# Transposes moved from TensorE to VectorE and block transfers in a two-layer hybrid trunk

## The chip, the cores and the metric

The kernel runs on one core of one Trainium2 chip. The metric is the device time of one execution in microseconds (us). Engines are called TensorE (PE in the profile; PEld is its weight load), VectorE (DVE), ScalarE (ACT), GpSimd (POOL) and SyncE (SP).

## The reference

The reference runs two layers over x, 256 tokens by 2048 channels, all in float32. Each layer computes, from one normalised input h:

```
h    = rms_norm(x) * norm_g
proj = h @ w_in                    # c_q, c_kv, k_rope, z_a, u, v, z_b, q_c, k_c, v_c, a_r, z_c, gates
y_a  = attention(c_q, c_kv, k_rope) * silu(z_a)   # 8 heads, 128 + 64 rotary, RMSNorm of q and k, causal softmax
y_b  = gelu(u) * (tril(w_s) @ rms_norm(gelu(v)) + b_s) * silu(z_b)   # inside chunks of 128 tokens
y_c  = rms_norm(gla(q_c, k_c, v_c, a_r)) * silu(z_c)   # gated linear attention, 4 heads, chunks of 128
merged = sum over the three branches of sigmoid(gate_b) * (y_b @ w_branch[b])
x    = x + merged @ w_out
```

## The kernel before

**Weights and blocks.** A projection block is 256 tokens by 512 output columns. Its contraction is cut into pieces of 128, and a weight chunk is two of these: 128 partitions by 1024 float32, 512 KB. `Weights.chunk` loads a chunk on SP's queue into `wraw` (four buffers), ScalarE rounds it into `whi` (L65), VectorE puts the rest into `wlo` (L66), three buffers each. `block` then makes three matmuls of 128x512 for each piece and each half of the tokens: high input by high weight (L207), high by low (L208), low by high (L209), so twelve to a chunk. The inputs need the same split: xT (the layer's input), cT (the normalised latents), yTa, yTb, yTc (the branch outputs) and mT (merged) all hold a transposed input in a high and a low half.

**A layer** runs through 320 chunks in this order: c_q and c_kv (32), z_a (32, behind a narrow block), q from cT0 (6), k and v of attention from cT1 (4 + 4), then q_c, k_c, v_c, z_c, v, u, z_b, the gates, the branch projections, and w_out. In the text these are counted as chunk positions from the layer's start: q begins at 34, the value block of attention ends at 48, q_c runs from 48 to 56, v begins at 96, u at 112. A layer has 320, so the second begins at 320.

**Transposes.** There are two ways to turn a block. `transpose_split` uses TensorE: `transpose2` (L242) makes four transposes of 128x128 into PSUM, ScalarE and VectorE split the result. Each block of 512 columns takes eight of them. `move_split`, used for the branch outputs, turns 32x32 squares on VectorE (L277, two instructions a block) and then moves the squares to their places with 16 transfers on SP's queue (L281, 32 KB each, 32 partitions by 8 runs of 128 bytes). Attention turns its queries and keys with `transpose2` as well, into qTn and kTn (heads' 128 columns), qTr (rotary queries) and kTz (rotary keys, zero in the other half of the partitions); so does the gated linear attention for qkT.

**Work between the matmuls.** Short pieces of work (transposes, attention, the gated linear attention) are written as generators in a list; `block` calls `step()` after every three matmuls, which carries the first piece on to its next `yield`. `pause(n)` lets n steps go by. A scheduler then settles each engine's order from the program order and from priorities; weight loads and splits have a raised priority. Every engine, and every queue of transfers, takes its instructions in that order, and one that waits holds up those behind it.

**Names that the text uses.** `attention` makes `scores` (psc, from kTz with qTr and kTn with qTn), `turn` and `values`. `rsqrt` (L124 on VectorE makes m, L126 on GpSimd makes r by a power) makes the norms r_q and r_k. krs is the rotary key scaled by r_k. `gla` has eight levels: VectorE's `factors` makes X, TensorE's `plv` multiplies its halves, VectorE writes the result into AT; `po` is its output.

Of the kernel before, what the change touches and what calls it, by code (L numbers as in the profile page):

```python
# [71 lines left out]
def trunk(ctx: ExitStack, tc: tile.TileContext, a, out):  # L72
# [252 lines left out]
    for l in range(DEPTH):  # L325
# [101 lines left out]
        qn = t8("qn").rearrange("p (t c) -> p t c", t=NT)  # L427
        qr = t4("qr").rearrange("p (t c) -> p t c", t=NT)
        for j in range(3):
            acc = block(lq, 4)  # L430
            for t in range(NT):
                dst = qn[:, t, j * 512:(j + 1) * 512] if j < 2 else qr[:, t, :]
                act(dst, acc[t], AF.Copy, scale=rc[:, t:t + 1])
        kn = t8("kn").rearrange("p (t c) -> p t c", t=NT)
        vv = t8("vv").rearrange("p (t c) -> p t c", t=NT)
        for j in range(4):
            acc = block(lk, 4)
            for t in range(NT):
                dst = (kn if j < 2 else vv)[:, t, (j % 2) * 512:(j % 2 + 1) * 512]
                act(dst, acc[t], AF.Copy, scale=rc[:, 2 + t:3 + t])  # L440
        ssq, ssk = ts("ssq", 32), ts("ssk")
        for t in range(NT):
            for src, dst in ((qn, ssq[:, t * 8:(t + 1) * 8]), (kn, ssk[:, t * 8:(t + 1) * 8])):
                sq = t4("sq")
                act(sq, src[:, t, :], AF.Square)
                V.tensor_reduce(dst, sq.rearrange("p (h d) -> p h d", h=NH), AX.X, ALU.add)
            sq = t2("sqr")
            act(sq, qr[:, t, :], AF.Square)
            V.tensor_reduce(ssq[:, 16 + t * 8:16 + (t + 1) * 8], sq.rearrange("p (h d) -> p h d", h=NH),
                            AX.X, ALU.add)  # L450
            V.tensor_scalar(ssk[:, t * 8:(t + 1) * 8], ssk[:, t * 8:(t + 1) * 8], sskr[:, t:t + 1], None, ALU.add)
        V.tensor_tensor(ssq[:, 0:16], ssq[:, 0:16], ssq[:, 16:32], ALU.add)
        rq = rsqrt(ssq[:, 0:16], 16, 1.0 / 192, "q")
        rk = rsqrt(ssk[:, 0:16], 16, 1.0 / 192, "k")
        rqs = ts("rqs")
        V.tensor_scalar(rqs, rq, SCALE, None, ALU.mult)

# [467 lines left out]
```

## Time and profile before

| | |
|---|---|
| time, median of 3 runs | 1863.21 us (1862.96 to 1863.21) |
| the profiled execution | 1863.55 us, of which the span of the core's instructions 1861.8 us |
| mean granted TensorE clock | 1.0 |
| TensorE matmul / weight load busy | 99% / 83% |
| VectorE / ScalarE / GpSimd busy | 60% / 50% / 2% |
| mean traffic of the transfers | 194 GB/s |

Busy shares are means over the span. TensorE takes its matmuls one after the other, and a record's duration overlaps the next one's start; so what a group of matmuls costs is read from the distance between starts. Instructions that issue a transfer are not counted as busy, on GpSimd and SyncE neither.

### The profile page before, as it was taken

The page shows a single profiled execution, that of the slowest core. Times are in us where ns is not written, and L with a number is a line of the kernel's source. Part 1 is how long each engine was busy: PE and PEld are TensorE (multiplying, and loading weights), DVE is VectorE, ACT ScalarE, POOL GpSimd, SP SyncE. Part 2 cuts the span into 40 slices and gives each one's busy share as a digit, 9 for nine tenths or more (in the row PEclk, how much of TensorE's full clock was granted, in tenths as well). Part 3 has the DMA queues.
Part 4 walks back from the last instruction along what each step waited for, and adds up shares of the span by engine and source line. Part 5 has one row for each costly group of instructions (what it writes and reads, how often), then busy time and mean ns, then how long its engine had stood idle before and what let it go on. Part 6 is the DMA issues. An engine that isn't in the chain of part 4 may idle for free.

```text
span 1861.8 us, 22708 instructions
## 1 busy us (share of the span) xinstructions
PE 1850.6 (99%) x8504; PEld 1537.8 (83%) x8504; DVE 1107.8 (60%) x1436; ACT 932.2 (50%) x1174; POOL 43.6 (2%) x49
## 2 busy tenths in 40 slices
PE   8999999999999999999999999999999999999999
PEld 7888888888888888888888888888888888888887
DVE  5656558866455545465556665688664555554654
ACT  6765446554444444444547644455544444444443
POOL 0002000000000000000000010000000000000000
PEclk9999999999999999999999999999999999999999
DMA  8554564475576555575655545645755765556654
GB/s 319 188 189 156 175 209 170 147 214 183 192 209 199 192 192 192 192 235 195 212 197 185 192 146 183 205 167 158 214 176 196 211 199 190 194 187 207 220 201 158
DMA packets 150607, 360.51 MB, mean 194 GB/s; under 512 B 63456, under 2 KB 64128, under 8 KB 149984
## 3 DMA queue, kind: packets, MB, share of 16 engines
q1 hardware_dynamic: 146400, 346.30, 56.0%
q0 software_dynamic: 2656, 10.37, 1.7%
q10 hardware_dynamic: 1440, 2.39, 0.4%
q8 instruction: 66, 1.08, 0.2%
q14 instruction: 45, 0.37, 0.1%
HBM read 348.52 MB, written 4.19 MB: 189 GB/s over the span
## 4 chain that ended last, share of the span: by engine, by line
PE 96%; DVE 1%; issue 1%; ACT 1%; POOL 1%; DMA 0%; ACTq 0%; DVEq 0%
PE acc L208 30%; PE acc L207 30%; PE acc L209 30%; PE ptr L242 2%; PE plv L670 1%; DVE wlo L66 1%; PE ppv L555 1%; PE psc L524 1%; PE psc L520 1%; POOL r_q L126 1%; PE pmx L767 0%; PE po L693 0%; PE ppt L545 0%; DMA first_in<-in_gx 0%; PE accT L221 0%
## 5 line engine op out<-in xcount | busy, mean ns | idle before, releaser
L66 DVE TENSOR_TENSOR wlo<-wraw,whi 128x1024 fp32r<-128x1024 f32 (+1 forms) x642 | 782.3, 1219 | 682.2 <-ACT whi L65 681.6
L65 ACT ACTIVATE whi<-wraw 128x1024 fp32r<-128x1024 f32 (+1 forms) x642 | 677.8, 1056 | 787.0 <-PE acc L209 762.6
L207 PE MATMUL acc<-whi,xT 128*128 128x512 f32 x1792 | 704.0, 393 | 5.8 <-ACT whi L65 5.8
L208 PE MATMUL acc<-wlo,xT 128*128 128x512 f32 x1792 | 699.6, 390 | 1.5 <-DVE wlo L66 1.4
L209 PE MATMUL acc<-whi,xT 128*128 128x512 f32 x1792 | 698.6, 390 | 0.0
L207 PEld LDWEIGHTS acc<-whi,xT 128*128 128x128 f32 x1792 | 337.1, 188 | 73.7 <-ACT whi L65 5.8
L208 PEld LDWEIGHTS acc<-wlo,xT 128*128 128x128 f32 x1792 | 337.2, 188 | 71.5 <-DVE wlo L66 3.8
L209 PEld LDWEIGHTS acc<-whi,xT 128*128 128x128 f32 x1792 | 337.0, 188 | 70.0
L207 PE MATMUL acc<-whi,mT 128*128 128x512 f32 x256 | 100.0, 391 | 0.0
L209 PE MATMUL acc<-whi,mT 128*128 128x512 f32 x256 | 99.7, 389 | 0.0
L208 PE MATMUL acc<-wlo,mT 128*128 128x512 f32 x256 | 99.6, 389 | 0.0
L209 PEld LDWEIGHTS acc<-whi,mT 128*128 128x128 f32 x256 | 48.1, 188 | 10.1
L207 PEld LDWEIGHTS acc<-whi,mT 128*128 128x128 f32 x256 | 48.1, 188 | 9.8
L208 PEld LDWEIGHTS acc<-wlo,mT 128*128 128x128 f32 x256 | 48.1, 188 | 9.8
L207 PE MATMUL acc<-whi,yTa 128*128 128x512 f32 x128 | 50.0, 390 | 0.0
L209 PE MATMUL acc<-whi,yTa 128*128 128x512 f32 x128 | 49.8, 389 | 0.0
L208 PE MATMUL acc<-wlo,yTa 128*128 128x512 f32 x128 | 49.8, 389 | 0.0
L207 PE MATMUL acc<-whi,yTb 128*128 128x512 f32 x128 | 49.8, 389 | 0.0
L208 PE MATMUL acc<-wlo,yTb 128*128 128x512 f32 x128 | 49.8, 389 | 0.0
L209 PE MATMUL acc<-whi,yTb 128*128 128x512 f32 x128 | 49.8, 389 | 0.0
L207 PE MATMUL acc<-whi,yTc 128*128 128x512 f32 x128 | 49.8, 389 | 0.0
L208 PE MATMUL acc<-wlo,yTc 128*128 128x512 f32 x128 | 49.8, 389 | 0.0
(236 smaller groups left out, 1439.9 us busy)
## 6 DMA issues: line engine op xcount, KB each, us to landing
wraw<-in_w_big SPq DMA_DIRECT2D x634, 512.0 KB, 3.3
whole<-part SPq DMA_DIRECT2D x192, 32.0 KB, 3.3
x<-x POOLq DMA_DIRECT2D x8, 512.0 KB, 4.4
x<-in_x SPq DMA_DIRECT2D x2, 1024.0 KB, 8.9
wsT<-in_w_sT POOLq DMA_DIRECT2D x2, 1024.0 KB, 5.7
x<-in_x POOLq DMA_DIRECT2D x4, 512.0 KB, 5.3
out<-x ACTq DMA_DIRECT2D x8, 256.0 KB, 4.7
xTraw<-in_gx SPq DMA_DIRECT2D x3, 512.0 KB, 7.6
```

The costliest lines, as they stand in the source:

```text
L65: nc.scalar.activation(hi[:, c], raw[:, c], AF.Copy)
L66: nc.vector.tensor_tensor(lo[:, c], raw[:, c], hi[:, c].bitcast(F32), ALU.subtract)
L126: nc.gpsimd.tensor_tensor(r[:, :n], m[:, :n], neghalf[:, :n], ALU.pow)
L207: nc.tensor.matmul(o, xh[:, c], wh, start=kt + k == 0, stop=False)
L208: nc.tensor.matmul(o, xh[:, c], wl, start=False, stop=False)
L209: nc.tensor.matmul(o, xl[:, c], wh, start=False, stop=kt + k == kts - 1)
L242: nc.tensor.transpose(p[:, k * S + t * P:k * S + (t + 1) * P], src[:, t, (b + k) * P:(b + k + 1) * P], ident)
L520: nc.tensor.matmul(p3[:, :, 0:nk], qTr[:, c:c + P], z[:, h0 % 4:h0 % 4 + 2, 0:nk], start=True, stop=False)
L524: nc.tensor.matmul(p3[:, k, 0:nk], qTn[:, h * S + i * P:h * S + (i + 1) * P], kTn[:, h * S:h * S + nk], start=False, stop=k == 1)
L555: nc.tensor.matmul(po[:, (h - hh) * P:(h - hh + 1) * P], pT[:, k:k + P], vv[:, j, h * P:(h + 1) * P], start=j == 0, stop=j == i)
L670: nc.tensor.matmul(p[:, h * P:(h + 1) * P], X[:, 0, h, :], X[:, 1, h, :], start=True, stop=True)
```

## The change

All `transpose_split` blocks but two kinds are replaced by moves: VectorE's two transposes and 16 transfers. A new helper `move` does this with the queue as a parameter. cT0, cT1, mT0 to mT2 of each layer, xT0 to xT2 of the second layer, and qkT go by SP's queue; qTn, qTr, kTz and kTn of attention by GpSimd's. The last merged block (mT3) and the last input block (xT3) stay on TensorE. q, k and v of attention are evicted in another order of code, the rotary keys lie in kTz0 (even heads) and kTz1 (odd heads), the rotary part of a score pair is two matmuls of half the width, and qTn is scaled in place by ScalarE before the first score. Attention's generator begins with `pause(48)` instead of the transposes, the pairs run through the first four heads first, and the branch and gate weights are laid out in the order gate0, gate1, branch0, branch1, gate2, branch2, gate3, branch3. The `squares` helper holds the sums of squares that stood in line before.

```diff
@@ -266,22 +266,32 @@
         work.append(steps())
         return dst
-    def move_split(src, scale, name):
-        dst, part, whole = t8(name, F32R), t4("part"), t4("whole")
-        dv = dst.rearrange("p (h n) -> p h n", h=2)
-        blocks = part.rearrange("p (n i b) -> p n i b", n=8, i=4)
-        w4 = whole.rearrange("p (n j b) -> p n j b", n=8, j=4)
+    def move(dst, src, queue=nc.sync):
+        part = t4("part")
         for t in range(NT):
             V.transpose(part.rearrange("p (k t c) -> p k t c", k=4, t=NT)[:, :, t, :],
                         src[:, t, :].rearrange("p (k c) -> p k c", k=4))
+        pv = part.rearrange("p (n i b) -> p n i b", n=8, i=4)
+        dst = dst if isinstance(dst, list) else [dst, dst]
+        dv = [d.rearrange("p (n j b) -> p n j b", n=8, j=4) for d in dst]
         for j in range(4):
             for i in range(4):
-                nc.sync.dma_start(w4[32 * i:32 * i + 32, :, j, :], blocks[32 * j:32 * j + 32, :, i, :])
-        for k in range(4):
-            c = slice(k * S, (k + 1) * S)
-            split(dv[:, 0, c], dv[:, 1, c], whole[:, c], scale(k) if callable(scale) else scale)
+                queue.dma_start(dv[i // 2][32 * i:32 * i + 32, :, j, :], pv[32 * j:32 * j + 32, :, i, :])
+    def move_split(src, scale, name):
+        dst, whole = t8(name, F32R), t4("whole")
+        dv = dst.rearrange("p (h n) -> p h n", h=2)
+        move(whole, src)
+        if callable(scale):
+            for k in range(4):
+                c = slice(k * S, (k + 1) * S)
+                split(dv[:, 0, c], dv[:, 1, c], whole[:, c], scale(k))
+        else:
+            split(dv[:, 0], dv[:, 1], whole, scale)
         return dst
@@ -362,7 +372,7 @@
-        cT = [transpose_split(cl[j], lambda k, j=j: gain(l, 16 + 4 * j + k), f"cT{j}") for j in range(2)]
+        cT = [move_split(cl[j], lambda k, j=j: gain(l, 16 + 4 * j + k), f"cT{j}") for j in range(2)]
@@ -465,49 +446,81 @@
...
+        qkg = ts("qkg", 1)
+        V.tensor_tensor(qkg, gain(l, 24), gain(l, 25), ALU.mult)
+        qn = t8("qn").rearrange("p (t c) -> p t c", t=NT)
+        qr = t4("qr").rearrange("p (t c) -> p t c", t=NT)
+        qTn = t8("qTn")
+        for j in range(3):
+            acc = block(lq, 4)
+            for t in range(NT):
+                dst = qn[:, t, j * 512:(j + 1) * 512] if j < 2 else qr[:, t, :]
+                act(dst, acc[t], AF.Copy, scale=rc[:, t:t + 1])
+            if j < 2:
+                move(qTn[:, j * 1024:(j + 1) * 1024], qn[:, :, j * 512:(j + 1) * 512], nc.gpsimd)
...
+        qrr, qrt = t4("qrr"), t4("qrt")
         rotate(v4(qrr), v4(qrt), qr.rearrange("p t (h d) -> p t h d", h=NH), 0, NH)
+        qTr = t4("qTr")
+        move(qTr, qrr.rearrange("p (t c) -> p t c", t=NT), nc.gpsimd)
...
+        kn = t8("kn").rearrange("p (t c) -> p t c", t=NT)
+        for j in range(2):
+            acc = block(lk, 4)
+            for t in range(NT):
+                act(kn[:, t, j * 512:(j + 1) * 512], acc[t], AF.Copy, scale=rc[:, 2 + t:3 + t])
+        ssk = ts("ssk")
+        squares(ssk[:, 0:16], kn)
+        for t in range(NT):
+            V.tensor_scalar(ssk[:, t * 8:(t + 1) * 8], ssk[:, t * 8:(t + 1) * 8], sskr[:, t:t + 1], None, ALU.add)
+        rk = rsqrt(ssk[:, 0:16], 16, 1.0 / 192, "k")
+        rk4 = rk.rearrange("p (t h) -> p t h", t=NT)
         krs = t4("krs")
...
         V.tensor_tensor(v4(krs), v1(krr).broadcast_to([P, NT, NH, 64]),
                         rk4.unsqueeze(3).broadcast_to([P, NT, NH, 64]), ALU.mult)
...
+        kTz = [t4("kTz0"), t4("kTz1")]
+        nc.gpsimd.memset(kTz[0][64:128, :], 0.0)
+        nc.gpsimd.memset(kTz[1][0:64, :], 0.0)
+        move(kTz, krs.rearrange("p (t c) -> p t c", t=NT), nc.gpsimd)
+        kTn = t8("kTn")
+        for j in range(2):
+            half = kn[:, :, j * 512:(j + 1) * 512]
+            for t in range(NT):
+                kf = half[:, t, :].rearrange("p (h d) -> p h d", h=4)
+                V.tensor_tensor(kf, kf, rk4[:, t, 4 * j:4 * j + 4].unsqueeze(2).broadcast_to([P, 4, P]), ALU.mult)
+            move(kTn[:, j * 1024:(j + 1) * 1024], half, nc.gpsimd)
+        vv = t8("vv").rearrange("p (t c) -> p t c", t=NT)
+        for j in range(2):
+            acc = block(lk, 4)
+            for t in range(NT):
+                act(vv[:, t, j * 512:(j + 1) * 512], acc[t], AF.Copy, scale=rc[:, 2 + t:3 + t])
+        for j in range(2):
+            act(qTn[:, j * 1024:(j + 1) * 1024], qTn[:, j * 1024:(j + 1) * 1024], AF.Copy, scale=qkg)
         lsum = ts("lsum")
         ya = t8("ya").rearrange("p (t c) -> p t c", t=NT)
         def attention():
-            yield from pause(16)
-            for g in range(2):
-                b = 4 * g
-                z = kTz[g].rearrange("p (h s) -> p h s", h=4)
-                nc.gpsimd.memset(z[64:128, 0::2, :], 0.0)
-                nc.gpsimd.memset(z[0:64, 1::2, :], 0.0)
-                pq, pk = transpose2(qrr3, b // 2), transpose2(krs3, b // 2)
-                act(qTr[:, b // 2 * S:(b // 2 + 2) * S], pq, AF.Copy)
-                pk = pk.rearrange("p (h s) -> p h s", h=2)
-                V.tensor_copy(z[0:64, 0::2, :], pk[0:64])
-                act(z[64:128, 1::2, :], pk[64:128], AF.Copy)
-                yield
-                for b in (4 * g, 4 * g + 2):
-                    pq, pk = transpose2(qn, b), transpose2(kn, b)
-                    act(qTn[:, b * S:(b + 2) * S], pq, AF.Copy, scale=qkg)
-                    V.tensor_copy(kTn[:, b * S:(b + 2) * S], pk)
-                    yield
+            yield from pause(48)
             def scores(i, h0):
@@ -515,14 +528,13 @@
...
-                z = kTz[h0 // 4].rearrange("p (h s) -> p h s", h=4)
-                c = h0 // 2 * S + i * P
-                nc.tensor.matmul(p3[:, :, 0:nk], qTr[:, c:c + P], z[:, h0 % 4:h0 % 4 + 2, 0:nk],
-                                 start=True, stop=False)
+                c = h0 // 2 * S
                 for k in range(2):
                     h = h0 + k
+                    nc.tensor.matmul(p3[:, k, 0:nk], qTr[:, c + i * P:c + (i + 1) * P], kTz[k][:, c:c + nk],
+                                     start=True, stop=False)
                     nc.tensor.matmul(p3[:, k, 0:nk], qTn[:, h * S + i * P:h * S + (i + 1) * P],
-                                     kTn[:, h * S:h * S + nk], start=False, stop=k == 1)
+                                     kTn[:, h * S:h * S + nk], start=False, stop=True)
...
-            pairs = [(i, h) for i in range(NT) for h in (0, 2, 4, 6)]
+            pairs = [(i, h) for g in (0, 4) for i in range(NT) for h in (g, g + 2)]
@@ -607,6 +619,8 @@
+        for j in range(2):
+            move(qkT[:, j], qk[:, j])
@@ -622,11 +636,6 @@
-            for j in range(2):
-                ps = [transpose2(qk[:, j], hp * 2) for hp in range(2)]
-                for hp in range(2):
-                    act(qkT[:, j, hp * 512:(hp + 1) * 512], ps[hp], AF.Copy)
-                yield from pause(2)
@@ -801,18 +810,19 @@
                     else:
                         V.scalar_tensor_tensor(g[:, t, :], g[:, t, :], 1.0, acc[t], ALU.add, ALU.mult)
                         V.tensor_tensor(m[:, t, :], m[:, t, :], g[:, t, :], ALU.add)
-            mT.append(transpose_split(m, 0.5, f"mT{nb}"))
+            return m
         gate_block(0)
         finish()
         yT[1] = [move_split(uz[:, :, j * 512:(j + 1) * 512], 1.0, f"yTb{j}") for j in range(2)]
         gate_block(1)
-        merge_block(0)
+        for nb in range(2):
+            mT.append(move_split(merge_block(nb), 0.5, f"mT{nb}"))
         gate_block(2)
-        merge_block(1)
+        m = merge_block(2)
         gate_block(3)
-        merge_block(2)
-        merge_block(3)
+        mT.append(move_split(m, 0.5, "mT2"))
+        mT.append(transpose_split(merge_block(3), 0.5, "mT3"))
         lm = hl(mT)
@@ -833,7 +843,8 @@
-                xT.append(transpose_split(x, lambda k, l=l, nb=nb: gain(l + 1, 4 * nb + k), f"xT{nb}"))
+                turn = move_split if nb < 3 else transpose_split
+                xT.append(turn(x, lambda k, l=l, nb=nb: gain(l + 1, 4 * nb + k), f"xT{nb}"))
@@ -866,7 +877,7 @@
-        for f, nb in ((gate, 0), (gate, 1), (branch, 0), (gate, 2), (branch, 1), (gate, 3), (branch, 2), (branch, 3)):
+        for f, nb in ((gate, 0), (gate, 1), (branch, 0), (branch, 1), (gate, 2), (branch, 2), (gate, 3), (branch, 3)):
```

What the scheduler makes of it, at the places on which the times depend:

On TensorE, at the end of attention's value block, before (acc_1328 and acc_1329 are the q_c block, ptr a transposes' PSUM tile):

```order
L207 MATMUL acc_1328<-whi,xT_96 128x512
L208 MATMUL acc_1328<-wlo,xT_96 128x512
L209 MATMUL acc_1328<-whi,xT_96 128x512
L242 MATMUL ptr<-c_ident,qrr 128x128 x4
L242 MATMUL ptr<-c_ident,krs 128x128 x4
L207 MATMUL acc_1329<-whi,xT_96 128x512
L208 MATMUL acc_1329<-wlo,xT_96 128x512
L209 MATMUL acc_1329<-whi,xT_96 128x512
L242 MATMUL ptr<-c_ident,qn 128x128 x4
L242 MATMUL ptr<-c_ident,kn 128x128 x4
```

These stand inside the q_c block, and the first score comes behind them at chunk 53.75. On TensorE in the changed kernel (acc_1425 is the last value block, acc_1469 the first matmuls of q_c):

```order
L207 MATMUL acc_1425<-whi,cT_531 128x512
L208 MATMUL acc_1425<-wlo,cT_531 128x512
L209 MATMUL acc_1425<-whi,cT_531 128x512
L534 MATMUL psc<-kTz_1317,qTr 128x128
L207 MATMUL acc_1469<-whi,xT_94 128x512
L208 MATMUL acc_1469<-wlo,xT_94 128x512
L209 MATMUL acc_1469<-whi,xT_94 128x512
```

The transposes are gone, and the first score matmul (kTz_1317 is kTz0) stands at chunk 48.0, ahead of the whole q_c block; its three companions stand at chunk 60.25. The second layer has the same order.

On GpSimd, the stretch from the decay's bias (ba) to the spatial unit's gain (vg), before:

```order
L381 DMA ba<-in_b_a 128x512
L126 TENSOR_TENSOR r_q<-m_q,neghalf 128x16
L126 TENSOR_TENSOR r_k<-m_k,neghalf 128x16
L498 MEMSET kTz_1323 64x2x256
L499 MEMSET kTz_1323 64x2x256
L498 MEMSET kTz_1324 64x2x256
L499 MEMSET kTz_1324 64x2x256
L723 DMA vg<-in_v_g 128x1024
```

and in the changed kernel:

```order
L391 DMA ba<-in_b_a 128x512
L282 DMA qTn<-part 32x8x32 x32
L126 TENSOR_TENSOR r_q<-m_q,neghalf 128x16
L282 DMA qTr<-part 32x8x32 x16
L126 TENSOR_TENSOR r_k<-m_k,neghalf 128x16
L501 MEMSET kTz_1317 64x1024
L502 MEMSET kTz_1318 64x1024
L282 DMA kTz_1317<-part 32x8x32 x2
L282 DMA kTz_1318<-part 32x8x32 x2
L282 DMA kTz_1317<-part 32x8x32 x2
...
L282 DMA kTn<-part 32x8x32 x32
```

The 96 transfers of attention stand in one line on GpSimd, with r_q, r_k and two memsets between them; the last transfer into kTz0 is the 14th of kTz's 16.

On TensorE, the gated linear attention's levels in the changed kernel (acc_2946 and acc_2947 are the last part of the v block):

```order
L679 MATMUL plv<-X 128x128 x16
L209 MATMUL acc_2946<-whi,xT_97 128x512
L207 MATMUL acc_2947<-whi,xT_97 128x512
L208 MATMUL acc_2947<-wlo,xT_97 128x512
L209 MATMUL acc_2947<-whi,xT_97 128x512
L207 MATMUL acc_2946<-whi,xT_97 128x512
L208 MATMUL acc_2946<-wlo,xT_97 128x512
L209 MATMUL acc_2946<-whi,xT_97 128x512
L207 MATMUL acc_2947<-whi,xT_97 128x512
L208 MATMUL acc_2947<-wlo,xT_97 128x512
L209 MATMUL acc_2947<-whi,xT_97 128x512
L679 MATMUL plv<-X 128x128 x8
```

Levels 0 to 3 stand together at chunk 111.17 and levels 4 and 5 at 112.0; level 6 follows at 113.67, level 7 at 116.08. Before, the eight levels stood apart, one of four matmuls at a time, from chunk 100.75 to 110.08. VectorE's factors stand in the same stretch. SP has the 32 transfers of qkT at the loads of chunks 94 to 115.

On SyncE, the end of the first layer in the changed kernel (whole is the tile that a move fills, here of xT2):

```order
L64 DMA wraw<-in_w_big 128x1024
L282 DMA whole<-part 32x8x32
L64 DMA wraw<-in_w_big 128x1024
L282 DMA whole<-part 32x8x32 x3
L64 DMA wraw<-in_w_big 128x1024
L282 DMA whole<-part 32x8x32
L64 DMA wraw<-in_w_big 128x1024
L282 DMA whole<-part 32x8x32 x7
L64 DMA wraw<-in_w_big 128x1024 x4
```

Before, no transfer stood between the weight loads there. The seven last transfers of xT2 stand behind the load of chunk 330, whose buffer comes free when TensorE has done with chunk 323; the first matmul that needs xT2 is at chunk 324.0.

## Rows read from the trace of the kernel before

**Rows 1.** Page, part 1: busy time and share of each engine.

```profile
PE 1850.6 (99%) x8504; PEld 1537.8 (83%) x8504; DVE 1107.8 (60%) x1436; ACT 932.2 (50%) x1174; POOL 43.6 (2%) x49
```

**Rows 2.** Waits of TensorE: waiter, releaser: us in all, times, longest.

```profile
PE acc L208 <- DVE wlo L66: 1.4, 4, 0.4
```

**Rows 3.** Timeline of ScalarE: start, us, instruction [idle before, releaser].

```profile
109.72 0.69 ACT L433 ACTIVATE qn<-acc,r_c 128x512 f32<-128x512 f32 x1 [1.04 <-PE acc L209]
111.31 0.67 ACT L433 ACTIVATE qn<-acc,r_c 128x512 f32<-128x512 f32 x1
...
142.30 0.69 ACT L440 ACTIVATE vv<-acc,r_c 128x512 f32<-128x512 f32 x1 [0.98 <-PE acc L209]
```

**Rows 4.** Timeline of TensorE at an input block's transposes.

```profile
937.46 0.40 PE L209 MATMUL acc<-whi,xT 128*128 128x512 f32 x1
937.70 1.04 PE L242 MATMUL ptr<-c_ident,x 128*128 128x128 f32 x8
...
938.81 0.40 PE L208 MATMUL acc<-wlo,xT 128*128 128x512 f32 x1
```

**Rows 5.** Instructions of L242: xcount, ns min/median/max, first to last start.

```profile
L242 PE MATMUL ptr<-c_ident,merged x64: 272/272/273, 615.9 to 1774.1; 128*128 128x128 f32 x64
...
L242 PE MATMUL ptr<-c_ident,cq x32: 270/272/273, 53.6 to 983.9; 128*128 128x128 f32 x32
...
L242 PE MATMUL ptr<-c_ident,qrr x16: 270/272/273, 155.6 to 1086.9; 128*128 128x128 f32 x16
```

**Rows 6.** Groups of VectorE by form: xcount, busy us, mean ns, idle before.

```profile
L277 DVE STREAM_TRANSPOSE part<-ya 128x512 f32<-128x512 f32 x8 | 5.6, 695 | 0.1
```

**Rows 7.** Timeline of SyncE: issues of a load and of block transfers.

```profile
238.69 0.33 SPq L64 DMA_DIRECT2D wraw<-in_w_big  x1
239.07 1.89 SPq L281 DMA_DIRECT2D whole<-part  x3
```

**Rows 8.** Timeline of GpSimd.

```profile
56.59 0.56 POOL L381 DMA_DIRECT2D ba<-in_b_a  x1
...
140.71 4.98 POOL L126 TENSOR_TENSOR r_q<-m_q,neghalf 128x16 f32<-128x16 f32 x1 [83.56 <-DVE m_q L124]
145.67 2.89 POOL L126 TENSOR_TENSOR r_k<-m_k,neghalf 128x16 f32<-128x16 f32 x1
...
802.87 0.73 POOL L826 DMA_DIRECT2D x<-in_x  x1 [12.19 <-DVE merged L803]
814.00 1.59 POOL L826 DMA_DIRECT2D x<-in_x  x2 [10.40 <-PE acc L209]
```

**Rows 9.** Timeline of VectorE: a weight split, m_k.

```profile
141.66 1.22 DVE L66 TENSOR_TENSOR wlo<-wraw,whi 128x1024 fp32r<-128x1024 f32 x1
142.80 0.21 DVE L124 TENSOR_SCALAR m_k<-ssk 128x16 f32<-128x16 f32 x1
```

**Rows 10.** Page, part 6: transfers by issuer, xcount, KB each, us to landing.

```profile
whole<-part SPq DMA_DIRECT2D x192, 32.0 KB, 3.3
x<-x POOLq DMA_DIRECT2D x8, 512.0 KB, 4.4
```

**Rows 11.** TensorE's first matmuls; windows, the granted clock is third from last.

```profile
7.29 0.63 PE L209 MATMUL acc<-whi,xT 128*128 128x512 f32 x1
7.72 0.63 PE L208 MATMUL acc<-wlo,xT 128*128 128x512 f32 x1
...
5.80:8.00 2.20, 2.15 (x5) 1.74 (x6) 2.15 (x5) 2.12 (x5) 0.00 (x0) 1.00 0.93 318
```

**Rows 12.** VectorE's level work; windows there (PE, PEld, DVE, ACT, POOL busy).

```profile
305.65 0.42 DVE L654 TENSOR_TENSOR X<-bT 128x256 f32<-128x256 f32 x1
305.99 0.42 DVE L653 TENSOR_TENSOR X<-bT 128x256 f32<-128x256 f32 x1
...
312.00:352.00 40.00, 40.00 (x208) 33.84 (x208) 37.37 (x76) 22.16 (x26) 0.00 (x0) 1.00 0.48 168
```

**Rows 13.** Page, part 5: ScalarE's copy of a weight chunk.

```profile
L65 ACT ACTIVATE whi<-wraw 128x1024 fp32r<-128x1024 f32 (+1 forms) x642 | 677.8, 1056 | 787.0 <-PE acc L209 762.6
```

More of the change, by code (lines that the diff above doesn't have):

```diff
@@ L426, in trunk @@
         lq, lk = hl([cT[0]]), hl([cT[1]])
[L427 to L456, printed above, removed]
+        v4 = lambda ap: ap.rearrange("p (t h d) -> p t h d", t=NT, h=NH)
+        v1 = lambda ap: ap.rearrange("p (t h d) -> p t h d", t=NT, h=1)
         def rotate(dst, tmp, src, j, shape):
@@ L466, in rotate, with squares @@
             V.tensor_tensor(dst, dst, tmp, ALU.add)
-        qrr = t4("qrr")
-        qrt = t4("qrt")
-        v4 = lambda ap: ap.rearrange("p (t h d) -> p t h d", t=NT, h=NH)
+        def squares(dst, src):
+            for t in range(NT):
+                sq = t4("sq")[:, 0:src.shape[2]]
+                act(sq, src[:, t, :], AF.Square)
+                V.tensor_reduce(dst[:, t * 8:(t + 1) * 8], sq.rearrange("p (h d) -> p h d", h=NH), AX.X, ALU.add)
+        qkg = ts("qkg", 1)
+        V.tensor_tensor(qkg, gain(l, 24), gain(l, 25), ALU.mult)
@@ L471, in trunk @@
+        ssq = ts("ssq", 32)
+        squares(ssq[:, 0:16], qn)
+        squares(ssq[:, 16:32], qr)
+        V.tensor_tensor(ssq[:, 0:16], ssq[:, 0:16], ssq[:, 16:32], ALU.add)
+        rq = rsqrt(ssq[:, 0:16], 16, 1.0 / 192, "q")
+        rqs = ts("rqs")
+        V.tensor_scalar(rqs, rq, SCALE, None, ALU.mult)
+        qrr, qrt = t4("qrr"), t4("qrt")
         rotate(v4(qrr), v4(qrt), qr.rearrange("p t (h d) -> p t h d", h=NH), 0, NH)
+        qTr = t4("qTr")
+        move(qTr, qrr.rearrange("p (t c) -> p t c", t=NT), nc.gpsimd)
@@ L472, in trunk @@
         krr, krt = ts("krr", 128, 1), ts("krt", 128, 1)
-        v1 = lambda ap: ap.rearrange("p (t h d) -> p t h d", t=NT, h=1)
         rotate(v1(krr), v1(krt), v1(kr), 1, 1)
+        kn = t8("kn").rearrange("p (t c) -> p t c", t=NT)
[7 more added lines that the diff above has]
+            V.tensor_scalar(ssk[:, t * 8:(t + 1) * 8], ssk[:, t * 8:(t + 1) * 8], sskr[:, t:t + 1], None, ALU.add)
@@ L475, in trunk @@
+        rk = rsqrt(ssk[:, 0:16], 16, 1.0 / 192, "k")
+        rk4 = rk.rearrange("p (t h) -> p t h", t=NT)
         krs = t4("krs")
-        rk4 = rk.rearrange("p (t h) -> p t h", t=NT)
         V.tensor_tensor(v4(krs), v1(krr).broadcast_to([P, NT, NH, 64]),
                         rk4.unsqueeze(3).broadcast_to([P, NT, NH, 64]), ALU.mult)
-        kf = kn.rearrange("p t (h d) -> p (t h) d", h=NH)
-        V.tensor_tensor(kf, kf, rk.unsqueeze(2).broadcast_to([P, 16, P]), ALU.mult)
-        qkg = ts("qkg", 1)
@@ L483, in trunk @@
-        V.tensor_tensor(qkg, gain(l, 24), gain(l, 25), ALU.mult)
-        qrr3 = qrr.rearrange("p (t c) -> p t c", t=NT)
-        krs3 = krs.rearrange("p (t c) -> p t c", t=NT)
-        qTn, kTn = t8("qTn"), t8("kTn")
-        qTr, kTz = t4("qTr"), [t4("kTz0"), t4("kTz1")]
+        kTz = [t4("kTz0"), t4("kTz1")]
[3 more added lines that the diff above has]
+        kTn = t8("kTn")
@@ new lines, in trunk @@
+        for j in range(2):
[7 more added lines that the diff above has]
+            acc = block(lk, 4)
+            for t in range(NT):
+                act(vv[:, t, j * 512:(j + 1) * 512], acc[t], AF.Copy, scale=rc[:, 2 + t:3 + t])
```

## The prediction

> **What bounds the kernel now.** I read the page's busy times first. TensorE is busy 1850.6 of 1861.8 us, VectorE 60%, ScalarE 50%, GpSimd 2% [rows 1]. The next view, who waited for whom on PE, says that this busy time is not slack in disguise: after its start PE waits four times for a split weight, 1.4 us in all [rows 2]. So PE's own instruction stream is the time, and two things can change it: work taken off PE, and new places where PE, which takes its instructions in order, must wait.
>
> The evictions give a clock for the rest. The first query block leaves PE at 109.72 and the last value block at 142.30, twelve weight chunks later [rows 3]: 32.58 us for 144 matmuls, 2.72 us a chunk and 0.226 us a matmul.
>
> **What the change takes off PE.** Eight transposes stand between two matmuls that start at 937.46 and 938.81 [rows 4]. Without them these two matmuls need 2 x 0.226, so eight transposes cost 0.90 us. The trace has 256 of them: 64 for merged, 32 each for cq, qn, kn, qk and x, 16 each for qrr and krs [rows 5] (qn, kn, qk and x have rows like that of cq, krs one like that of qrr). Only the last merged block of each layer and the last x block stay (24), so 232, that is 29 groups, go: 29 x 0.90 = **-26.1 us**. The rotary score matmul is split in two of half the width, with the same columns: nothing. The new order of branch and gate blocks moves weights, not work: nothing.
>
> **What it adds beside PE.** There are 29 new block moves, each with two VectorE transposes of 0.695 us [rows 6], 40 us in all. VectorE is idle for 754 of the 1861.8 us, so I cost this at nothing except in the places below; if VectorE ran late everywhere, the weight splits behind would be late too, and PE has two or three chunks of split weights in hand against that. ScalarE loses the copies out of PSUM. SP gets 17 x 16 transfers; the order interleaves one to three of them with each weight load, as it already does for the branch outputs, where a transfer takes 0.63 us of SP and a load 0.33 [rows 7]. Two of these per chunk fit in 2.72 us.
>
> **First new wait: the first score.** In the new PE order the first score matmul stands right behind the last value block, twelve chunks ahead of the rest of that score, and it needs the last transfer into kTz0. All of PE's queue stands behind it. PE arrives there at 142.30 less 16 cq transposes (1.8): 140.5. When does kTz0 land? GpSimd issues everything in order:
> - The second part of the first query block is evicted by 111.98 [rows 3], now 110.2; with a VectorE transpose behind it (0.7), GpSimd starts at 110.9.
> - 32 transfers for qTn. No row shows GpSimd issuing a block transfer. The nearest are its x loads, which like a block transfer have 256 runs: 0.73 us, two in a row 1.59; its load with 128 runs takes 0.56 [rows 8]. I take 0.75, for the equal runs, and keep 0.54 and 1.0 as ends. 24.0, so 134.9.
> - r_q, 4.98 [rows 8]: 139.9. 16 transfers for qTr, 12.0: 151.9. r_k, 2.89: 154.8.
> - VectorE makes krs (two inputs over 1024, like the weight split's 1.22 in [rows 9]), scales half of kn (half of that, 0.6) and turns krs (1.4): 158.0, taken as 158.1. GpSimd's memsets run meanwhile.
> - 14 of kTz's 16 transfers, 10.5: 168.6. Landing: 3.3 us from issue for such a transfer from SP, 4.4 from GpSimd for a large one [rows 10]; I take 3.3, of which 0.75 is counted: 171.1.
>
> PE waits 30.6 us. In the second layer all stands alike: **+61 us**. Each 0.1 us on a transfer moves it by 62 x 0.1 x 2 = 12 us. At 0.54 the stall is about 20.5 a layer (GpSimd then waits a little for m_q), at 1.0 it is 46. No row below 0.54 is near, yet even at zero the chain r_k (2.89, after m_k at 143 as in [rows 9]), krs, turning and landing (3.2 + 3.3) ends near 152, 11 us late. What follows is not late: kTn's 32 transfers have the twelve chunks after it (32.6 us).
>
> The Trainium skill (SBUF — State Buffer, Who interferes with whom) speaks against issuing from GpSimd: its descriptors cannot be written while VectorE holds the shared port in a two-port mode. No row here shows such a delay: two x loads in a row took 1.59, twice the single one. By the rule the transfers under VectorE's work would take longer than 0.75 and the time would go towards the slow case below, 1966.
>
> **Restart.** After PE's idle start its matmuls began 0.43 us apart, not 0.226, while the granted clock of that stretch reads 1.00 [rows 11]. 0.43 is what 512 columns take at 1.2 GHz, the lower of the two levels. Twelve such cost 2.4 us. I count it for the two long stalls: **+5**. Between 0 and 10.
>
> **Second new wait: the GLA levels.** Before, q and k came from PE and the levels' VectorE work ran from 305 on, 37.4 us busy of 40 with PE full [rows 12]. Now qkT comes by 32 SP transfers spread over 21 chunks; the last lands about when VectorE reaches it, 14 chunks into the v block (chunk 110). The first four levels' matmuls are bunched there and most of the level work follows behind: up to level 7's last product 50 instructions of 256 columns at 0.34 (start to start, [rows 12]), five of 512 at twice that, five weight splits at 1.14 (start to start, [rows 9]): 17.0 + 3.4 + 5.7 = 26.1 us. PE has in that stretch 59 matmuls (13.3) and seven levels of eight small matmuls, each taken like eight transposes (0.9): 19.6. PE reaches the first level about 0.9 after VectorE begins (an estimate from the chunks between). So PE waits some 5.6 us a layer: **+11**. Between 0 (PE arrives later) and 20.
>
> **Third new wait: the layer boundary.** xT2 is moved by SP now. Its last seven transfers stand behind the weight load that waits for PE's chunk before the first one that needs xT2. From there: weight copy 1.06 [rows 13] and split 1.14, load 0.33, six transfers 3.8, landing 3.3, first split 0.5: **+10**, once. Between 5 (landing at the shortest, transfers overlapping) and 15.
>
> **Sum**, against the profiled execution's own 1863.55 (span 1861.8): 1863.55 - 26.1 + 61 + 5 + 11 + 10 = 1924.5. That execution is 0.3 above the median 1863.21, so I say **1924**.
>
> **Rivals.**
> - *Only the first score stalls* (13%). For it: VectorE and ScalarE have idle time, and their rows do overlap; against it: the order is fixed. 1863.55 - 26.1 + 61 + 5 = 1903, at 0.54 us a transfer 1883.
> - *GpSimd is slower* (13%). If each transfer waits for half of a running weight split (0.57) 60% of the time, it costs 0.75 + 0.34 = 1.1, and 62 x 0.34 x 2 = 42 us come on top: 1966. For it: r_q takes 4.98 and r_k 2.89 with the same shape [rows 8], so something holds GpSimd up at times. Against it: the x loads agree. This is how a delay of GpSimd's transfers by VectorE would show here; the Trainium skill's sentence above is about such a delay.
> - *The score does not wait* (7%). kTz0 lands before PE arrives, because transfers of 32 KB issue far faster than any row or because the r_k chain is early. Then 1863.55 - 26.1 + 21 = 1858, or 1837 if the other two waits are covered too. It comes out faster when the two kTz stalls together stay under 26 us with the other waits covered, or under 5 us with them as priced. Against it: the 11 us that are left at zero issue time.
> - *The order on the chip is not the program's*, or PE's pieces go ahead of a waiting one (1%): 1837. Against it: in the rows of PE before the matmuls stand in the program's order.
>
> **Numbers.** The forecast, all three waits with a transfer between 0.54 and 1.0, has 66%, since each of its three waits follows from the fixed order on PE; its own range is 1894 (1924 - 20 - 10) to 1961 (+31, and 6 for the other bounds). The range 1892 to 1962 holds it, nearly all of the first rival's half, and leaves out the slow GpSimd case and the gains. About 0.2% (3.7 us) is what a measurement can tell: the two cases without the long stall share 8 points, 5 of them faster by more than that and 3 within it (other waits as priced, 1858, with a little stall left); all else, 92%, is slower.
>
> **What would show it.** PE's waits should be led by L534, psc waiting for a DMA into kTz, near 30 us twice, and the chain of waits should run through GpSimd there. GpSimd's rows should show L282 back to back at about 0.75. PE should wait for X from VectorE at the GLA levels and for xT once in the middle of the run. 29 groups of L242 should be gone. The prediction is wrong if PE stays 99% busy, or if the L282 rows on GpSimd are near 0.3 or over 1.0.

## The result: 3% slower, at the time that was forecast

The changed kernel takes **1923.12 us** (median of 4 runs, 1922.32 to 1926.5) against 1863.17 us before: ratio 1.0325, 95% interval 1.0308 to 1.0343. The profiled execution took 1922.69 us, with a span of 1920.9 us. The forecast was 1924 us. The total is right, and the first score does stall as forecast, but the terms behind the total are off in both directions and cancel, so that it comes within 1 us is luck. This is told below.

The page of the changed kernel, part 1, answers to [rows 1]:

```profile
PE 1843.2 (96%) x8304; PEld 1528.0 (80%) x8304; DVE 1134.5 (59%) x1458; ACT 918.6 (48%) x1124; POOL 150.6 (8%) x237
```

GpSimd's 150.6 us do hold its issues of transfers (the 192 of L282 are 110.7 us of them), other than the remark on busy shares above says. The span grew by 59.1 us. TensorE's busy time fell by 7.4 us only (1850.6 to 1843.2); so its idle time grew by 66.5, from 11.2 to 77.7 us. Where it was idle stands in the view of PE's waits (waiter, releaser, us in all, times, longest); it answers to [rows 2]:

```profile
PE psc L534 <- DMA kTz<-part: 41.5, 2, 21.3
PE acc L207 <- ACT xT L229: 9.3, 1, 9.3
PE plv L679 <- DVE X L667: 9.2, 4, 2.9
PE acc L207 <- ACT whi L65: 5.6, 1, 5.6
PE acc L207 <- DVE sza L429: 4.0, 2, 3.1
PE acc L207 <- DVE vn L729: 3.2, 4, 1.1
PE acc L208 <- DVE wlo L66: 1.0, 3, 0.4
```

Five rows are new: the first score (41.5), the layer boundary (9.3), the levels (9.2), the first block of q in the first layer, which waits for cT0 although the profile names sza (4.0), and the matmuls behind the levels (3.2). They are 67.2 us together.

PE's timeline at the first of the two score stalls shows the wait and what follows it:

```profile
168.27 0.77 PE L534 MATMUL psc<-kTz,qTr 128*128 128x128 f32 x2 [20.13 <-DMA kTz<-part]
...
172.68 0.63 PE L207 MATMUL acc<-whi,xT 128*128 128x512 f32 x1
173.11 0.63 PE L208 MATMUL acc<-wlo,xT 128*128 128x512 f32 x1
...
174.21 0.39 PE L208 MATMUL acc<-wlo,xT 128*128 128x512 f32 x1
174.44 0.40 PE L209 MATMUL acc<-whi,xT 128*128 128x512 f32 x1
```

Until 173.96 the matmuls start 0.43 us apart, the distance of [rows 11]; from there on 0.23. The granted clock is the reason. In six stretches between PE's start and its end it reads 0.50, the lower of the two levels (1.2 GHz), and each begins in a wait of PE or just behind one: for cT0, the first score, the levels, the layer boundary, the second score and the levels again. Their windows (stretch, length, then PE, PEld, DVE, ACT and POOL busy; the clock is third from last):

```profile
105.73:112.55 6.82, 5.61 (x12) 4.00 (x13) 3.67 (x8) 1.71 (x4) 0.00 (x0) 0.50 0.23 77
150.10:173.99 23.89, 5.72 (x15) 4.59 (x16) 7.61 (x12) 1.45 (x3) 21.87 (x33) 0.50 0.36 82
371.96:378.79 6.83, 4.92 (x19) 4.49 (x20) 6.83 (x20) 3.88 (x6) 0.00 (x0) 0.50 0.23 77
976.12:986.37 10.25, 6.09 (x14) 4.85 (x15) 3.35 (x8) 3.81 (x9) 0.00 (x0) 0.50 0.16 27
1109.24:1129.72 20.48, 3.64 (x10) 3.00 (x11) 7.22 (x11) 0.00 (x0) 18.79 (x29) 0.50 0.28 55
1331.11:1337.94 6.83, 5.19 (x16) 4.52 (x17) 6.83 (x19) 4.06 (x7) 0.00 (x0) 0.50 0.06 25
```

PE is busy for 31.2 us in them. At 0.43 us in place of 0.227, some 0.47 of this is the price of the clock: about 15 us (an estimate from these rows). The 1.00 of [rows 11] is no reading: the clock's first record in the trace of the kernel before stands at 10.79 us, and there the distance falls from 0.43 to 0.23.

GpSimd's timeline in the first layer answers to [rows 8]. It is the chain that the prediction worked out:

```profile
118.78 9.23 POOL L282 DMA_DIRECT2D qTn<-part  x16 [61.97 <-DVE part L275]
128.66 8.04 POOL L282 DMA_DIRECT2D qTn<-part  x14 [0.65 <-DVE ssq L454]
136.89 1.16 POOL L282 DMA_DIRECT2D qTn<-part  x2 [0.19 <-issue]
138.06 2.93 POOL L126 TENSOR_TENSOR r_q<-m_q,neghalf 128x16 f32<-128x16 f32 x1
142.10 7.60 POOL L282 DMA_DIRECT2D qTr<-part  x13 [1.10 <-DVE part L275]
...
152.08 2.93 POOL L126 TENSOR_TENSOR r_k<-m_k,neghalf 128x16 f32<-128x16 f32 x1
...
158.38 5.81 POOL L282 DMA_DIRECT2D kTz<-part  x10 [1.37 <-DVE part L275]
164.49 3.46 POOL L282 DMA_DIRECT2D kTz<-part  x6 [0.30 <-issue]
```

A transfer costs GpSimd 0.58 us, at the low end of the forecast's bounds. Two rows tell of more than issue: GpSimd waits for VectorE ahead of qTr (1.10) and ahead of kTz (1.37).

At the layer boundary, SyncE's timeline answers to [rows 7]:

```profile
970.66 0.33 SPq L64 DMA_DIRECT2D wraw<-in_w_big  x1
971.04 0.59 SPq L282 DMA_DIRECT2D whole<-part  x1
973.38 0.33 SPq L64 DMA_DIRECT2D wraw<-in_w_big  x1
973.76 4.50 SPq L282 DMA_DIRECT2D whole<-part  x7
```

The seven last transfers of xT2 go out from 973.76 on, behind a weight load. PE had run out at 971.0 and went on at 980.28.

### The profile page after: what moved, and what is told of

Its sections match the earlier page's. It is cut to its first block, busy times and chain, and to the rows that moved or that the text cites. A ratio compares the mean times of both kernels' runs of the same rounds, so it can differ in the third digit from the quotient of the medians.

```text
span 1920.9 us, 22960 instructions
## 1 busy us (share of the span) xinstructions
PE 1843.2 (96%) x8304; PEld 1528.0 (80%) x8304; DVE 1134.5 (59%) x1458; ACT 918.6 (48%) x1124; POOL 150.6 (8%) x237
## 4 chain that ended last, share of the span: by engine, by line
PE 90%; DVE 4%; POOL 2%; DMA 2%; issue 1%; ACT 1%; SPq 0%; ACTq 0%; POOLq 0%; DVEq 0%
PE acc L208 29%; PE acc L207 29%; PE acc L209 29%; DVE wlo L66 1%; DMA whole<-part 1%; POOL kTz L282 1%; PE plv L679 1%; PE psc L534 1%; PE ppv L567 1%; PE psc L536 1%; ACT whi L65 0%; DVE part L275 0%; DVE yc L714 0%; POOL r_k L126 0%; PE pmx L776 0%
## 5 line engine op out<-in xcount | busy, mean ns | idle before, releaser
L534 PE MATMUL psc<-kTz,qTr 128*128 128x128 f32 (+1 forms) x64 | 16.4, 339 | 41.5 <-DMA kTz<-part 41.5
```

The source lines that it names most:

```text
L534: nc.tensor.matmul(p3[:, k, 0:nk], qTr[:, c + i * P:c + (i + 1) * P], kTz[k][:, c:c + nk], start=True, stop=False)
```

## The experiments

All are edits of the changed kernel (1923 us) or of an earlier experiment, and each is compared with the kernel before on its own chip.

### The score pair in the other order

```diff
-                    nc.tensor.matmul(p3[:, k, 0:nk], qTr[:, c + i * P:c + (i + 1) * P], kTz[k][:, c:c + nk],
-                                     start=True, stop=False)
                     nc.tensor.matmul(p3[:, k, 0:nk], qTn[:, h * S + i * P:h * S + (i + 1) * P],
-                                     kTn[:, h * S:h * S + nk], start=False, stop=True)
+                                     kTn[:, h * S:h * S + nk], start=True, stop=False)
+                    nc.tensor.matmul(p3[:, k, 0:nk], qTr[:, c + i * P:c + (i + 1) * P], kTz[k][:, c:c + nk],
+                                     start=False, stop=True)
```

> The changed kernel with the two matmuls of a score pair in the other order: the kTn part first (it opens the sum), the kTz part behind it. The first score then stands at chunk 60.25, with the rest of its pair, and nothing of attention at 48.0. Theory (the stall comes from the early place of one matmul, and the transfers themselves are early enough for chunk 60): both kTz waits (41.5 us) and the slow matmuls behind them (about 4.5) go: 1922.7 - 46 = 1877 us. PE comes to 60.25 at about 181, the first half of kTn lands at about 180. Rival (GpSimd's queue is late for any place): the wait moves to 60.25, up to 8 us a layer, because all of kTn lands only at about 189: 1894. Second rival (PE's waiting was no loss): 1923.

Measured: 1898.19 us, ratio 1.0186 (1.0169 to 1.0203). The score waits are gone from PE's list, and neither the score nor kTn appears there; so the early place of one matmul made the 41.5 us, and the transfers are early enough for chunk 60. But 25 us were gained, not 46 (29 in the profiled execution, at 1893.36 the fastest of the four). PE's waits in this kernel show why:

```profile
PE acc L208 <- DVE wlo L66: 11.3, 5, 5.8
PE acc L207 <- ACT xT L229: 9.4, 1, 9.4
PE plv L679 <- DVE X L667: 8.2, 4, 2.9
...
PE acc L207 <- ACT vv L516: 3.4, 2, 1.7
```

And VectorE's timeline there:

```profile
149.32 1.23 DVE L66 TENSOR_TENSOR wlo<-wraw,whi 128x1024 fp32r<-128x1024 f32 x1 [0.26 <-ACT whi L65]
155.96 1.23 DVE L495 TENSOR_TENSOR krs<-krr,r_k 128x1024 f32<-128x1024 f32 x1 [5.41 <-POOL r_k L126]
157.10 0.68 DVE L509 TENSOR_TENSOR kn<-kn,r_k 128x512 f32<-128x512 f32 x1
...
161.88 1.30 DVE L275 STREAM_TRANSPOSE part<-kn 128x512 f32<-128x512 f32 x2
163.10 3.45 DVE L66 TENSOR_TENSOR wlo<-wraw,whi 128x1024 fp32r<-128x1024 f32 x3
```

VectorE stands 5.4 us in front of krs, waiting for r_k, which waits on GpSimd behind qTr's transfers. Between the splits at 149.32 and 163.10 it makes no weight split, and PE runs dry. The score stall had hidden this: while PE stood, nobody needed splits. Neither rival of the expectation named it. In the profiled execution the missing 17 us are these waits (10.3 more than in the changed kernel), two for ScalarE's eviction of vv (3.4) and about 3 us of slow matmuls behind them.

### The transfers of q left out

```diff
-                move(qTn[:, j * 1024:(j + 1) * 1024], qn[:, :, j * 512:(j + 1) * 512], nc.gpsimd)
+                V.tensor_copy(qTn[:, j * 1024:(j + 1) * 1024].rearrange("p (t c) -> p t c", t=NT), qn[:, :, j * 512:(j + 1) * 512])
-        move(qTr, qrr.rearrange("p (t c) -> p t c", t=NT), nc.gpsimd)
+        V.tensor_copy(qTr, qrr)
```

> The changed kernel without the 32 transfers of qTn and the 16 of qTr: VectorE copies the untransposed queries into these tiles in place of turning them (the transposition of q is left out). GpSimd keeps r_q, r_k, kTz and kTn, and the first score stays at chunk 48.0. The forecast's sum (the stall is GpSimd's serial issue of 62 transfers): 48 x 0.58 = 27.7 us less a layer, so no stall, 1923 - 46 = 1877 us. Theory after the trace (r_k can't start before m_k at 149.1, where GpSimd was held by qTr only until 152.1; then come krs, its turning, 14 transfers of kTz and their landing): only 3 us a layer are gained, the stall stays at 17 us, 1923 - 6 = 1917 us.

Measured: 1918.78 us, ratio 1.0296 (1.028 to 1.0311). With 48 of the 62 transfers gone the two stalls are 16.66 and 17.86 us, 34.5 in place of 41.5. GpSimd's timeline, and PE's row of the first score:

```profile
139.40 3.30 POOL L126 TENSOR_TENSOR r_q<-m_q,neghalf 128x16 f32<-128x16 f32 x1 [82.29 <-DVE m_q L124]
151.59 2.90 POOL L126 TENSOR_TENSOR r_k<-m_k,neghalf 128x16 f32<-128x16 f32 x1 [8.89 <-DVE m_k L124]
...
158.40 9.41 POOL L282 DMA_DIRECT2D kTz<-part  x16 [1.90 <-DVE part L275]
...
168.13 0.76 PE L534 MATMUL psc<-kTz,qTr 128*128 128x128 f32 x2 [16.66 <-DMA kTz<-part]
```

GpSimd now stands idle for 8.89 us until VectorE has m_k. So the keys' own chain (their eviction, squares, m_k, r_k, krs, turning, kTz) is nearly as late as the queue: q's transfers add only 3.5 us a layer to the stall. In the first layer even this is not an earlier landing. The score starts at 168.13 (168.27 in the changed kernel), but PE arrives 3.3 us later, at 151.5, after a longer wait for cT0 (1.1), more slow matmuls behind it and a wait for wlo (0.7), and the keys are later with it. In the second layer PE takes as long from the first stall to the second as before (936 us), and there the landing itself is earlier.

### qTn issued from ScalarE

```diff
-                move(qTn[:, j * 1024:(j + 1) * 1024], qn[:, :, j * 512:(j + 1) * 512], nc.gpsimd)
+                move(qTn[:, j * 1024:(j + 1) * 1024], qn[:, :, j * 512:(j + 1) * 512], nc.scalar)
```

> The changed kernel with the 32 transfers of qTn issued from ScalarE's queue; qTr, kTz and kTn stay on GpSimd, and the first score stays at chunk 48.0. The forecast's sum (GpSimd is busy without a gap from the first transfer to the last of kTz): 32 x 0.58 = 18.5 us a layer less, the stall falls from 20-21 to about 2 us, 1923 - 37 = 1886. Theory after the trace (GpSimd had been waiting for VectorE before qTr; from there the chain is qTr's transfers, r_k, krs, its turning and kTz): the stall stays at 19 to 21 us, time 1920 to 1926, more if ScalarE's weight copies get late behind 32 issues.

Measured: 1962.41 us (two runs), ratio 1.053 (1.0509 to 1.0551). The score waits are 42.9 us in all, as the second theory had it, but this run is not clean: ScalarE's issues hold up its own evictions, and PE gets two new waits.

```profile
PE acc L207 <- ACT kn L487: 14.1, 2, 7.1
PE acc L207 <- ACT qn L465: 13.5, 2, 6.8
```

The keys are late by the same amount then, so the unchanged stall proves nothing here; the run above settles the point. What this one shows is the price of the other queue: 39 us for issuing 32 transfers a layer from an engine that feeds PE.

### qkT on TensorE again

```diff
-        for j in range(2):
-            move(qkT[:, j], qk[:, j])
...
+            for j in range(2):
+                ps = [transpose2(qk[:, j], hp * 2) for hp in range(2)]
+                for hp in range(2):
+                    act(qkT[:, j, hp * 512:(hp + 1) * 512], ps[hp], AF.Copy)
+                yield from pause(2)
```

> The changed kernel with qkT turned on TensorE again, as before (4 groups of eight transposes, +3.6 us); all else as changed. Theory (qkT's 32 transfers, paced by SP's weight loads, land late and bunch the levels): the levels go back to chunks 100.75 to 110, the waits for X (9.2) and for vn behind them (3.2) and the slow small matmuls there (about 5) go: 1922.7 - 17.4 + 3.6 = 1909 us. Rival (VectorE has simply too much to do there): waits for X stay, 1923 to 1926.

Measured: 1906.73 us, ratio 1.0229 (1.0214 to 1.0244). Both rows, plv's wait for X and acc's wait for vn, are gone from PE's list. Sixteen us are back for four groups of transposes that cost 3.6; the second stall was made by qkT's late landing, not by VectorE's load. This edit also takes four turns a layer (2.8 us) off VectorE; but in the run with all moves from GpSimd, below, VectorE makes them still, and both rows are gone there too.

### xT on TensorE again

```diff
-                turn = move_split if nb < 3 else transpose_split
+                turn = move_split if nb < 0 else transpose_split
```

> The changed kernel with xT0 to xT2 of the second layer turned on TensorE again (three groups, +2.7 us). Theory (xT2's last transfers stand behind SP's weight load that waits for PE): the wait of 9.3 us at the layer boundary and the slow matmuls there (3.1) go: 1922.7 - 12.4 + 2.7 = 1913 us. Rival (the second layer waits for the last block's norm or its x anyway): 1923 to 1926.

Measured: 1916.16 us, ratio 1.0282 (1.0267 to 1.0297). The 9.3 us row is gone. The gain is 6.9 us, with 2.7 for the three groups in it, so 9.6 of the 12.4 expected: the wait for cT0 took 4.9 us in this profile, 0.9 more, and the slow matmuls behind it some 1.3 more.

### cT from GpSimd

```diff
-        cT = [move_split(cl[j], lambda k, j=j: gain(l, 16 + 4 * j + k), f"cT{j}") for j in range(2)]
+        cT = [move_split(cl[j], lambda k, j=j: gain(l, 16 + 4 * j + k), f"cT{j}", nc.gpsimd) for j in range(2)]
```

(`move_split` hands the queue on to `move`.)

> The changed kernel with the moves of cT0 and cT1 issued from GpSimd, all else as changed. Theory (in the first layer cT0's transfers, paced by SP's weight loads, land 4 us late; all of attention's chain begins with q, so it moves forward as well): 1922.7 - 4.0 - 2.3 = 1916.4 us, the kTz waits stay at 20 to 21 us. Rival (kTz's landing is fixed by something else): the kTz wait of the first layer grows by what is gained, 1922 to 1923.

Measured: 1920.63 us, ratio 1.0309 (1.0294 to 1.0324). The wait named after sza is gone and the score stalls stay (20.09 and 20.91), so the theory holds for them. The time does not show it: 2.5 us were gained of the 6.3 forecast, and the intervals of the two kernels overlap. A new row stands in the list:

```profile
PE pk L403 <- ACT kr L406: 3.6, 1, 3.6
```

ScalarE's timeline has the reason: it waits 4.27 us for the transfers into cT1's tile, whose split stands ahead of kr's eviction.

```profile
73.75 1.30 ACT L229 ACTIVATE cT<-whole,first_in 128x256 fp32r<-128x256 f32 x3 [4.27 <-DMA whole<-part]
...
77.25 0.30 ACT L406 ACTIVATE kr<-pk,r_x 128x64 f32<-128x64 f32 x1
```

### All moves from GpSimd

The score order of the first experiment, cT as above, xT0 to xT2 from GpSimd in the same way, and qkT's moves on GpSimd, written right behind the evictions of q_c and k_c:

```diff
                 act(qk[:, j, t, :], acc[t], AF.Copy, scale=col(scal["dk"] if j == 0 else r, t))
+        qkT = t8("qkT").rearrange("p (j n) -> p j n", j=2)
+        for j in range(2):
+            move(qkT[:, j], qk[:, j], nc.gpsimd)
```

> The changed kernel with the score pair's order as in e1_swap, and the moves of cT, qkT and xT issued from GpSimd too, qkT right behind q_c and k_c. The same transposes are off TensorE (29 groups). Theory (the four waits come from one early matmul and from moves that stand between SP's weight loads; GpSimd has room): all four go, 1863.5 - 26.1 = 1837 to 1842 us. Rival (GpSimd's single queue gets the new bound: 13 - 3 moves a layer in one line, a late kTn or qkT stops PE): 1850 to 1880.

Measured: 1861.04 us (10 runs), ratio 0.9992 (0.9979 to 1.0005): no difference from before. The boundary, the levels, the scores and cT0 are gone from PE's list, as the theory had it, but the time is 19 us above its 1842. The rival's range holds the time and its wait is not in the list, neither for kTn nor for qkT. What is left, beside the start, is mostly the wait for splits, which stand behind VectorE's wait for r_k (6.63 us here) as in the first experiment:

```profile
PE acc L208 <- DVE wlo L66: 13.2, 2, 7.0
...
PE acc L207 <- ACT vv L516: 3.4, 2, 1.7
PE pk L403 <- ACT kr L406: 1.6, 1, 1.6
```

### r_k ahead of qTr

Two edits, made once on the kernel with the other score order (e11) and once on the one with all moves from GpSimd (g4):

```diff
-        move(qTr, qrr.rearrange("p (t c) -> p t c", t=NT), nc.gpsimd)
...
         move(kTz, krs.rearrange("p (t c) -> p t c", t=NT), nc.gpsimd)
+        move(qTr, qrr.rearrange("p (t c) -> p t c", t=NT), nc.gpsimd)
...
-            yield from pause(48)
+            yield from pause(64)
```

> e1_swap with two more edits: the move of qTr is written behind that of kTz, so that r_k stands ahead of qTr's 16 transfers on GpSimd, and attention pauses for 64 steps, not 48, so that the later qTr and kTn are still in time (first score at about chunk 64). Theory (in e1_swap VectorE waits 5.4 us for r_k in front of krs, the weight splits queue behind krs, and PE waits 5.8 and 4.7 us for wlo): that wait and the slow matmuls behind it (1.7 a layer) go: 1898 - 14 = 1884 us. Rival (kn's scaling and turning alone keep VectorE from the splits): 3 to 5 us a layer stay, 1890. Second rival (the wait moves to the score, for kTn or qTr): 1890 to 1898.

Measured: 1891.87 us, ratio 1.0146 (1.0129 to 1.0163). Of the wait for wlo 11.3 us became 5.2; 1.99 and 2.27 stay at the two places. VectorE's wait for r_k is 3.0 us now, not 5.4, and between its splits at 155.04 and 161.54 stand a turn of qrr and all the scaling and turning of kn. That is the first rival: its time (1890) is met, with waits of half its size and slow matmuls behind them.

> g2_all_pool_early with the same two edits as e11_swap_rk. Theory: of g2's time, 13.2 us of waits for wlo and 4.4 us of slow matmuls behind them go: 1861 - 17.6 = 1843 us, and PE's remaining waits are the start's and two for vv. Rival (GpSimd, now the issuer of 12 moves a layer in one line, lands kTn or qkT late): a wait for kTn or qkT of 3 to 8 us a layer, 1850 to 1860.

Measured: **1850.68 us**, ratio 0.9937 (0.9918 to 0.9956), 12.6 us below the kernel before and 72 below the changed one. PE's list:

```profile
PE acc L208 <- DVE wlo L66: 4.1, 2, 2.0
PE pk L403 <- ACT kr L406: 4.0, 1, 4.0
PE acc L207 <- ACT vv L516: 3.4, 2, 1.7
```

The theory was 8 us too low: 4.1 us of the wait for wlo stay, and the wait for kr grew from 1.6 to 4.0. The rival's range holds this time too, but no wait for kTn or qkT is in the list.

```diff
+        cg = lambda k, j: gain(l, 16 + 4 * j + k)
-        cT = [move_split(cl[j], lambda k, j=j: gain(l, 16 + 4 * j + k), f"cT{j}", nc.gpsimd) for j in range(2)]
+        cT = [transpose_split(cl[j], lambda k, j=j: cg(k, j), f"cT{j}") if l == 0 else
+              move_split(cl[j], lambda k, j=j: cg(k, j), f"cT{j}", nc.gpsimd) for j in range(2)]
```

> g4_rk_first with cT0 and cT1 of the first layer turned on TensorE again (two groups of eight transposes, +1.8 us); the second layer's stay with GpSimd. Theory (in g4 ScalarE stands at cT1's split until the transfers have landed, the evictions of kr queue behind it and PE waits 4.0 us for kr, with 2.2 us of slow matmuls behind): 1850.7 - 6.2 + 1.8 = 1846 us. Rival (kr is late for another reason, the rotary tables on VectorE): the wait stays, 1852 us.

Measured: 1852.39 us (5 runs, 1850.93 to 1853.68), ratio 0.994 (0.9928 to 0.9953). The wait for kr is gone, as the theory had it, but not the time: two groups of transposes came back (1.8), PE now waits 1.6 us for x at the boundary, and slow matmuls (1.6) appear in the second layer, where the granted clock reads 0.50 (1074.51 to 1077.92) behind a wait of 2.03 us. In g4 the clock stays at 1.00 behind the same wait; why it fell here is not shown. The better version stays the one above.

## Why the prediction was right

**The transposes** (-26.1). Not measured alone. With PE's list nearly empty (g4), the span is 1849.7, 12.1 below the 1861.8 of before, while PE's waits after its start are 11.7 us (4.1, 4.0, 3.4 and a row of 0.2) in place of 1.4. PE's busy time is 1828.0 there, 22.6 below before; about 2 us more of slow matmuls than before are in it: about -25, near the forecast. In the changed kernel, with 15 us of slow matmuls in PE's busy time, it is about -22.

**The first score** (+61, measured 41.5). The mechanism, the place and the number of stalls are as forecast; the size is not. In the first layer PE came at 148.1 and not 140.5, mostly because of the wait for cT0 (6.5 us with its slow matmuls) that the forecast did not have. This changed little in the stall, since GpSimd's line began later by as much (118.8, not 110.9), and the run without that wait still has a stall of 20.09. The 10.5 us between 30.6 and 20.1 lie in the chain. The transfer cost 0.58 us, not 0.75, which is 10.5 us for 62 of them; the choice among the bounds went to the row with equal runs, and the row with half of them (0.56) was the nearer. r_q took 2.9 in place of 5.0, and the landing 1.9 from issue in place of 3.3; against these two stand about 3 us in which GpSimd waited between its transfers. And "GpSimd issues everything in order", taken as the only bound, is wrong: the line of 62 transfers is nearly unbroken in the trace, but r_k could not have started before m_k at 149.1, 3 us sooner than it did, and without 48 of the transfers the stall is 17 us still. The slope of 12 us for each 0.1 us a transfer held down to 0.58 and would have misled below it; there the sentence that even at zero issue time 11 us remain was nearer to the cause than the sum was.

**The restart** (+5, between 0 and 10). At the two score stalls it is right: 12 and 7 matmuls at 0.43, 2.5 and 1.5 us above 0.227. But the step "I count it for the two long stalls" failed. The clock fell behind shorter waits as well: at cT0 (2.5 us), the boundary (2.9) and the levels, where eight plv records take 2.05 in place of 1.05. TensorE's busy time fell by 7.4 and not by 26.1; of the 18.7 us between, about 15 are the six stretches at the lower clock, 10 more than forecast, and 3 to 4 are not assigned.

**The levels** (+11). The waits for X are 9.2 and those for vn behind them 3.2, with about 5 us of slow matmuls at the lower clock there: some 17. The run with qkT on TensorE gained 16.4 with 3.6 of transposes in it, so 20; of the rest, 1.4 are fewer slow matmuls at the boundary and 0.5 shorter score stalls, and about 1 is not assigned. Place and cause are as forecast.

**The boundary** (+10). 9.3, as forecast, plus 2.9 of slow matmuls, which belong to the restart.

**Not seen**: cT0 in the first layer (4.0 and 2.5; the wait is 4.0 to 5.0 in the runs that leave it as it is). Its transfers are spread one or two to a weight load like qkT's, and the forecast priced them at nothing with "two of these per chunk fit in 2.72 us". They fit; they are late all the same, since the last of them waits for the last of those loads.

So the sum came out by offset, which is luck: 19.5 us too much for the score against some 10 too little for the restart, 4 for cT0, 3 to 4 for what PE saved less, and 1 to 2 for the levels. Of the rivals, that only the score stalls fell with the rows of the levels and the boundary. GpSimd slowed by VectorE did not occur either: its transfers took 0.58 to 0.66 us each in every trace, with VectorE busy beside them. The Trainium skill (SBUF — State Buffer, Who interferes with whom) warns of GpSimd's descriptors waiting for VectorE's two-port operations; no run here shows it, and two thirds of VectorE's time beside these transfers (44 of 66 us in the changed kernel) is of the two-input form, for which the page names no two-port mode. So the prediction was wrong to apply the rule to all of VectorE's work, and this case hardly tests it.

## What to carry to other kernels

When work leaves the engine that bounds a kernel, look for the first instruction on that engine that needs the moved result, and for its place in the order: here one matmul that was issued twelve chunks early made 41.5 us of waits, and the order of two lines undid them, for 25 us of the time; the rest came back as waits that the stall had hidden. Price the chain of the data as well as the queue of the issuer, and follow every in-order engine that waits on that chain (VectorE for r_k, ScalarE for cT1), because its other work feeds the bound engine. Transfers that share a queue with loads which wait for buffers move at the pace of these loads; put them on a queue whose engine feeds few others, and ahead of them what it does feed (here r_k).
